# Layer norm of a two-block network: one DVE pass becomes an ACT pass and a POOL product, and an rms scaling goes from POOL to ACT

## The chip, the core and the metric

The kernel runs on one core of a Trainium2 chip. Its time is the device time of one execution in microseconds (us), the median of several runs. The core's engines each work through their own list of instructions in a fixed order and meet by semaphores: TensorE (PE; its weight loads are shown apart as PEld), VectorE (DVE), ScalarE (ACT), GpSimd (POOL) and SyncE (SP), which issues the DMAs.

## What is computed

A sequence of 1024 tokens with 1024 channels, and a context of 256 tokens, go through a "first block" of two layers and then through a "second block". Each layer of the first block projects the tokens, mixes them in three ways (a short convolution, a retention, a windowed attention), multiplies the mixed channels by `w_out`, adds the result, gated, to the scaled input, and takes a layer norm:

```python
def layer_norm(x, g, b):
    xf = x.astype(F32)
    mu = jnp.mean(xf, axis=-1, keepdims=True)
    var = jnp.mean(jnp.square(xf - mu), axis=-1, keepdims=True)
    return ((xf - mu) * lax.rsqrt(var + LN_EPS) * g + b).astype(x.dtype)

x_new = layer_norm(DEEPNORM_ALPHA * x + gate[:, None] * y, ln_g, ln_b)
```

Layer 0 does this for the 1024 tokens and for the 256 context tokens, layer 1 for the 1024 tokens alone. The second block starts with an rms norm of the result, `xf * rsqrt(mean(xf * xf) + RMS_EPS) * g`, and a projection of it.

## The kernel before

Tokens lie in tiles of 128 (partitions) by 1024 (channels), named `tok`: tiles 0 to 3 make group 0, tiles 4 to 7 group 1, and in layer 0 the two context tiles 8 and 9 group 2. Every matmul is made of three fp32r products of high and low halves (`hi`, `lo`); the high half is a copy on ACT or POOL (L211, L213), the low half a difference on DVE (L214, L738).

The stage in question is `p4`. It multiplies by `w_out` in two column halves (`ch`). For each half and each token tile, PE runs 24 matmuls of 128x512 into one PSUM tile `pp` (there are four in rotation); DVE then multiplies by the gate (L1422), adds the scaled input (L1423) and takes the half's statistics (L1429). After the second half `norm` finishes a tile: DVE aggregates mean and variance (L1430), POOL forms `rs`, the inverse root, in two small instructions (L467, L468), and DVE makes two passes over the whole tile (L1432, L1434). `then` stores the tile (`X<-tok`, on SP's queue); in layer 1 it also calls `rms_tok`: a sum of squares on ACT (L754), again L467 and L468 on POOL, and a scaling of the tile in place, on POOL (L1576).

When the last tile of a group is done, `transposes` is put on a background list. Its steps are handed out between matmuls: PE transposes the group's four tiles, one block of 128 channels at a time (four matmuls on L685 into half of a PSUM tile `S`; two such tiles in rotation). Below, k0 to k7 are the eight blocks of a group. In layer 0 ACT evacuates each block with an affine map (L742, into `hv`), POOL makes the high half (L211) and DVE the low half (L214). In layer 1 ACT makes the high half from PSUM (L737) and DVE the low half (L738). A transpose into the second half of an `S` tile waits until the first half has been read: by L742 in layer 0, by L738 in layer 1. `hv` shares its two buffers with the output of L1422.

A scheduler writes each engine's list from the program; within a list the order is fixed.

Of the kernel before, what the change touches and what calls it, by code (L numbers as in the profile page):

```python
# [9 lines left out]
AF = mybir.ActivationFunctionType  # L10
ALU = mybir.AluOpType
# [127 lines left out]
class Kern:  # L139
# [1263 lines left out]
    def p4(s, l, groups, rows):  # L1403

        nc, W = s.nc, s.A["w_out"][l]
        rr = {}
        for ch in range(2):
            wt = s.want("r", W, 0, 8, ch * 512, 512)
            c = slice(ch * 512, (ch + 1) * 512)
            for gi, (act, xsrc, gate, then) in enumerate(groups):  # L1410
                nt = len(xsrc)
                if ch == 0:
                    rr[gi] = [s.tokt() for _ in range(nt)]
                    for t in range(nt):
                        s.load(rr[gi][t], xsrc[t])
                    if not rows:
                        rows += [s.row(s.A["ln_g"][l:l + 1]), s.row(s.A["ln_b"][l:l + 1])]
                r = rr[gi]

                def ev(t, ps):  # L1420
                    y = s.norm.tile([128, 512], F32, tag="hv", name="gy", bufs=2)
                    nc.vector.tensor_tensor(out=y, in0=ps, in1=gate[:, c], op=ALU.mult)  # L1422
                    nc.vector.scalar_tensor_tensor(out=r[t][:, c], in0=r[t][:, c], scalar=ALPHA, in1=y,  # L1423
                                                   op0=ALU.mult, op1=ALU.add)

                def norm(t):
                    st, mv, rs = s.small(12, "bn"), s.small(2, "mv"), s.small(1, "ln")
                    for j in range(2):
                        nc.vector.bn_stats(out=st[:, 6 * j:6 * j + 6], in_=r[t][:, j * 512:(j + 1) * 512])  # L1429
                    nc.vector.bn_aggr(out=mv, in_=st.rearrange("p (j c) -> p j c", j=2))  # L1430
                    s.pow_m05(rs, mv[:, 1:2], 1, 1.0, LN_EPS)
                    nc.vector.scalar_tensor_tensor(out=r[t], in0=r[t], scalar=mv[:, 0:1], in1=rows[0],  # L1432
                                                   op0=ALU.subtract, op1=ALU.mult)
                    nc.vector.scalar_tensor_tensor(out=r[t], in0=r[t], scalar=rs, in1=rows[1], op0=ALU.mult,  # L1434
                                                   op1=ALU.add)
                    then(r, t)
                end = ch == 1 and gi == len(groups) - 1
                s.tm(wt, [(act, t * 128) for t in range(nt)], 512, ev, post=norm if ch else None,
                     outer="t")
# [133 lines left out]
    def rms_tok(s, x):  # L1573

        rs = s.rstd_rms([x], [s.norm.tile([128, 1024], F32, tag="junk", name="junk", bufs=1)])
        s.nc.gpsimd.tensor_scalar(out=x, in0=x, scalar1=rs, scalar2=1.0, op0=ALU.mult, op1=ALU.mult)  # L1576


    def second_block(s, h):
# [505 lines left out]
```

## Time and profile before

| | |
|---|---|
| runs of the kernel before | 3041.79 us median of 3 (3033.36 to 3044.56) |
| the profiled execution | 3042.17 us, of which 3040.0 us lie between its first and last instruction |
| PE, PEld | busy 97% and 80% of the span |
| DVE, ACT, POOL | busy 60%, 34% and 24% |
| `p4` of layer 0, second column half | begins near 786 us; its tiles are done near 877 us |
| `p4` of layer 1, second column half | begins near 1467 us; its tiles are done near 1540 us |
| L1432 and L1434 | 18 instructions each (10 tiles in layer 0, 8 in layer 1) |
| L1576 | 8 instructions |

The profile shows one execution. Times count from the start of its span. An engine's idle time is put down to what released it; a "wait" is idle time before an instruction, with the engine and line that ended it.

### The profile page before, as it was taken

Reading aid. Unit: us, or ns where it says so; the run is one execution under the profiler, and the core shown is the slowest. Engines: PE = TensorE matmul, PEld = TensorE weight load, DVE = VectorE, ACT = ScalarE, POOL = GpSimd, SP = SyncE. Lnnn points to the kernel's source line nnn. Section 1 sums busy time; section 2 is a strip of 40 time slices with the busy share of each in tenths; the row PEclk is TensorE's granted clock in tenths of the full one; section 3 lists DMA queues with packets and bytes.
Section 4 is the critical chain, followed back from the end, with each engine's and each line's share of the span. In section 5 each row is a group of like instructions: output and inputs, shape, how many; then the busy total and the mean of one; then the engine's idle time right before and its main releaser. Section 6 shows DMA issues by size and latency. Waiting matters only on the chain. (4 is left out here: it accounts for less than half of the span.)

```text
span 3040.0 us, 40710 instructions
## 1 busy us (share of the span) xinstructions
PE 2934.0 (97%) x15449; PEld 2445.2 (80%) x15449; DVE 1823.8 (60%) x2813; ACT 1044.3 (34%) x1822; POOL 719.5 (24%) x742
## 2 busy tenths in 40 slices
PE   7989999999999999999999999999899999999989
PEld 5978887787789997887778878788778888887877
DVE  4555643445865644445752376884448877778965
ACT  3222223234122323234121152533454443444462
POOL 3222221121233222121310021212143332224130
PEclk9999999999999999999999999999999999999999
DMA  7273434333433223333312222165453332267554
GB/s 265 60 187 96 120 114 110 112 84 101 168 97 110 83 67 95 89 84 106 140 57 70 87 75 82 63 224 204 137 183 106 116 121 88 84 229 258 172 201 137
DMA packets 343603, 378.47 MB, mean 124 GB/s; under 512 B 30916, under 2 KB 258416, under 8 KB 343408
## 3 DMA queue, kind: packets, MB, share of 16 engines
q1 hardware_dynamic: 343408, 375.87, 39.0%
q8 instruction: 122, 2.00, 0.3%
q14 instruction: 73, 0.60, 0.1%
HBM read 303.11 MB, written 68.76 MB: 122 GB/s over the span
## 5 line engine op out<-in xcount | busy, mean ns | idle before, releaser
L308 PE MATMUL pp<-act_hi,whi 128*128 128x512 f32 (+1 forms) x1472 | 576.1, 392 | 1.6 <-POOL whi L211 1.0
L308 PE MATMUL pp<-act_hi,wlo 128*128 128x512 f32 (+1 forms) x1472 | 562.8, 383 | 1.7 <-DVE wlo L214 1.7
L308 PE MATMUL pp<-act_lo,whi 128*128 128x512 f32 (+1 forms) x1472 | 561.5, 382 | 1.0 <-DVE act_lo L1662 1.0
L214 DVE TENSOR_TENSOR wlo<-wr,whi 128x1024 fp32r<-128x1024 f32 (+2 forms) x304 | 335.1, 1116 | 348.7 <-ACT whi L213 174.7
L308 PE MATMUL pp<-whi,act_hi 128*128 128x384 f32 (+1 forms) x1216 | 446.7, 368 | 26.4 <-ACT pl L1895 9.1
L308 PE MATMUL pp<-wlo,act_hi 128*128 128x384 f32 (+1 forms) x1216 | 442.5, 364 | 4.6 <-DVE wlo L214 4.6
L308 PE MATMUL pp<-whi,act_lo 128*128 128x384 f32 (+1 forms) x1216 | 437.9, 360 | 0.0
L211 POOL TENSOR_SCALAR whi<-wr 128x1024 fp32r<-128x1024 f32 (+2 forms) x128 | 147.3, 1151 | 861.5 <-PE pp L308 610.1
L308 PEld LDWEIGHTS pp<-act_hi,whi 128*128 128x128 f32 x1472 | 278.3, 189 | 73.7 <-issue 20.3
L308 PEld LDWEIGHTS pp<-act_hi,wlo 128*128 128x128 f32 x1472 | 278.7, 189 | 57.3 <-issue 2.7
L308 PEld LDWEIGHTS pp<-act_lo,whi 128*128 128x128 f32 x1472 | 279.1, 190 | 51.0 <-issue 2.5
L213 ACT ACTIVATE whi<-wr 128x1024 fp32r<-128x1024 f32 (+2 forms) x176 | 152.8, 881 | 354.5 <-PE pp L308 267.1
L308 PEld LDWEIGHTS pp<-whi,act_hi 128*128 128x128 f32 x1216 | 231.6, 191 | 51.8 <-issue 11.1
L308 PEld LDWEIGHTS pp<-wlo,act_hi 128*128 128x128 f32 x1216 | 232.3, 191 | 28.0 <-DVE wlo L214 10.3
L308 PEld LDWEIGHTS pp<-whi,act_lo 128*128 128x128 f32 x1216 | 231.7, 191 | 18.0
L1360 POOL TENSOR_SCALAR P<-P,sm 128x640 f32<-128x640 f32 x96 | 76.4, 810 | 223.7 <-DVE sm L1358 223.7
L374 PE MATMUL pp<-act,wx 128*128 128x512 f32 x320 | 124.6, 389 | 0.0
L377 PE MATMUL pp<-act,wx 128*128 128x512 f32 x320 | 124.5, 389 | 0.0
L376 PE MATMUL pp<-act,wx 128*128 128x512 f32 x320 | 124.5, 389 | 0.0
L2036 PE MATMUL pp<-whi,act 128*128 128x512 f32 x384 | 121.5, 394 | 0.0
L1356 ACT ACTIVATE P<-P,sm 128x640 f32<-128x640 f32 x96 | 79.0, 824 | 121.2 <-DVE sm L1354 121.1
L96 POOL TENSOR_TENSOR ws<-wr 128x512 f32<-128x512 f32 x48 | 66.8, 1392 | 153.5 <-DMA wr<-in_w_up_dram 142.8
(378 smaller groups left out, 5237.6 us busy)
## 6 DMA issues: line engine op xcount, KB each, us to landing
wr<-in_w_in_dram SPq DMA_DIRECT2D x40, 768.0 KB
wr<-in_w_up_dram SPq DMA_DIRECT2D x56, 512.0 KB
wr<-in_w_in_dram SPq DMA_DIRECT2D x52, 512.0 KB
wr<-in_w_down_dram SPq DMA_DIRECT2D x21, 1024.0 KB
act<-HID SPq DMA_DIRECT2D x84, 256.0 KB
wr<-in_w_in_dram SPq DMA_DIRECT2D x19, 1024.0 KB
wr<-in_w_mod_dram SPq DMA_DIRECT2D x16, 1024.0 KB
wr<-in_w_out_dram SPq DMA_DIRECT2D x12, 1024.0 KB
```

Of the source, the lines that this page charges most:

```text
L96: s.K.nc.gpsimd.tensor_tensor(out=t, in0=a, in1=b, op=op)
L211: nc.gpsimd.tensor_scalar(out=hi, in0=src, scalar1=1.0, scalar2=0.0, op0=ALU.mult, op1=ALU.add)
L213: nc.scalar.activation(out=hi, in_=src, func=AF.Copy)
L214: nc.vector.tensor_tensor(out=lo, in0=src, in1=hi.bitcast(F32), op=ALU.subtract)
L308: s.nc.tensor.matmul(out=ps, lhsT=lhs[a], rhs=rhs[b], start=first and n == 0, stop=last and n == 2)
L374: s.nc.tensor.matmul(out=ps, lhsT=x[0][:, k], rhs=y[k][0], start=first and k == 0, stop=False, skip_group_check=True)
L376: s.nc.tensor.matmul(out=ps, lhsT=x[0][:, k], rhs=y[k][1], start=False, stop=False, skip_group_check=True)
L377: s.nc.tensor.matmul(out=ps, lhsT=x[1][:, k], rhs=y[k][0], start=False, stop=last and k == 3, skip_group_check=True)
L1356: nc.scalar.activation(out=P[:, hh], in_=P[:, hh], func=AF.Exp, scale=-1.0, bias=m[:, hh:hh + 1], accum_out=sm[:, hh:hh + 1])
L1360: nc.gpsimd.tensor_scalar(out=P[:, hh], in0=P[:, hh], scalar1=sm[:, hh:hh + 1], scalar2=0.5, op0=ALU.mult, op1=ALU.mult)
L2036: nc.tensor.matmul(out=ps[t], lhsT=a[:, c], rhs=b, start=own and k == 0 and n == 0, stop=k == KT - 1 and n == 2, skip_group_check=True)
```

## The change

In `norm` the two DVE passes become four steps. A small DVE instruction forms `mr = -mean * rs` (L1433 of the changed kernel); ACT computes `r * rs + mr` over the tile (L1435); POOL multiplies by the row `ln_g` (L1436); DVE adds the row `ln_b` (L1437). All three passes work in place. In `rms_tok` the scaling of the tile moves from POOL to ACT (L1578).

```diff
                     s.pow_m05(rs, mv[:, 1:2], 1, 1.0, LN_EPS)
-                    nc.vector.scalar_tensor_tensor(out=r[t], in0=r[t], scalar=mv[:, 0:1], in1=rows[0],
-                                                   op0=ALU.subtract, op1=ALU.mult)
-                    nc.vector.scalar_tensor_tensor(out=r[t], in0=r[t], scalar=rs, in1=rows[1], op0=ALU.mult,
-                                                   op1=ALU.add)
+                    mr = s.small(1, "mr")
+                    nc.vector.scalar_tensor_tensor(out=mr, in0=mv[:, 0:1], scalar=-1.0, in1=rs, op0=ALU.mult,
+                                                   op1=ALU.mult)
+                    nc.scalar.activation(out=r[t], in_=r[t], func=AF.Identity, scale=rs, bias=mr)
+                    nc.gpsimd.tensor_tensor(out=r[t], in0=r[t], in1=rows[0], op=ALU.mult)
+                    nc.vector.tensor_tensor(out=r[t], in0=r[t], in1=rows[1], op=ALU.add)
                     then(r, t)
...
         rs = s.rstd_rms([x], [s.norm.tile([128, 1024], F32, tag="junk", name="junk", bufs=1)])
-        s.nc.gpsimd.tensor_scalar(out=x, in0=x, scalar1=rs, scalar2=1.0, op0=ALU.mult, op1=ALU.mult)
+        s.nc.scalar.activation(out=x, in_=x, func=AF.Copy, scale=rs)
```

The lists of DVE, ACT and POOL change around these steps. First DVE, in the run of tiles 1 to 5 of either layer, where one tile's rows repeat for the next. Before, from the statistics of one tile to those of the next:

```order
L1430 BN_AGGR sm<-sm 128x2
L1432 SCALAR_TENSOR_TENSOR tok<-tok,sm,row 128x1024
L1434 SCALAR_TENSOR_TENSOR tok<-tok,sm,row 128x1024
L1422 TENSOR_TENSOR gy<-pp,row 128x512
L1423 SCALAR_TENSOR_TENSOR tok<-tok,gy 128x512
L1429 BN_STATS sm<-tok 128x6
L1430 BN_AGGR sm<-sm 128x2
```

Now:

```order
L1430 BN_AGGR sm<-sm 128x2
L1433 SCALAR_TENSOR_TENSOR sm<-sm 128x1
L1422 TENSOR_TENSOR gy<-pp,row 128x512
L1437 TENSOR_TENSOR tok<-tok,row 128x1024
L1423 SCALAR_TENSOR_TENSOR tok<-tok,gy 128x512
L1429 BN_STATS sm<-tok 128x6
L1430 BN_AGGR sm<-sm 128x2
```

Only L1422 of the next tile has come ahead of the finished tile's last pass L1437; L1423, L1429 and L1430 of the next tile stand behind it.

Second, ACT in layer 0, from the second column half of `p4` to the evacuation of group 0's transposes (`hv` is that evacuation, `whi` a weight's high half):

```order
-L742 ACTIVATE hv<-S,MODC_156 128x512 x4
+L1435 ACTIVATE tok<-tok,sm 128x1024 x5
+L742 ACTIVATE hv<-S,MODC_156 128x512
+L1435 ACTIVATE tok<-tok,sm 128x1024
+L742 ACTIVATE hv<-S,MODC_156 128x512 x3
```

The evacuation of block k0 now stands behind the affine pass of tile 4, and that of k1 to k3 behind the pass of tile 5.

Third, DVE in layer 1, where the low halves of group 0's blocks (`act_lo`) begin. Before:

```order
L1432 SCALAR_TENSOR_TENSOR tok<-tok,sm,row 128x1024
L1434 SCALAR_TENSOR_TENSOR tok<-tok,sm,row 128x1024
L738 SCALAR_TENSOR_TENSOR act_lo<-S,COL,act_hi 128x512
L1422 TENSOR_TENSOR gy<-pp,row 128x512
L1423 SCALAR_TENSOR_TENSOR tok<-tok,gy 128x512
L738 SCALAR_TENSOR_TENSOR act_lo<-S,COL,act_hi 128x512 x2
```

Now:

```order
L1433 SCALAR_TENSOR_TENSOR sm<-sm 128x1
L738 SCALAR_TENSOR_TENSOR act_lo<-S,COL,act_hi 128x512
L1437 TENSOR_TENSOR tok<-tok,row 128x1024
L738 SCALAR_TENSOR_TENSOR act_lo<-S,COL,act_hi 128x512 x2
L1422 TENSOR_TENSOR gy<-pp,row 128x512
```

The low half of k0 stands behind L1433 of tile 5 instead of L1434 of tile 5, and the low halves of k1 and k2 behind L1437 of tile 5.

## Rows read from the trace of the kernel before

**Rows 1.** The page, part 1: busy time, share and instructions by engine

```profile
PE 2934.0 (97%) x15449; PEld 2445.2 (80%) x15449; DVE 1823.8 (60%) x2813; ACT 1044.3 (34%) x1822; POOL 719.5 (24%) x742
```

**Rows 2.** Busy time by stretch: length, each engine's busy us (instructions), granted clock, DMA

```profile
800.00:820.00 20.00, 20.00 (x90) 16.54 (x89) 16.68 (x21) 0.00 (x0) 6.60 (x8) 1.00 0.20 80
```

**Rows 3.** Who waited for whom, 780 to 880 us: total us, times, longest

```profile
PE S L685 <- ACT hv L742: 5.0, 3, 1.8
```

**Rows 4.** The same view, 1465 to 1560 us

```profile
PE S L685 <- DVE act_lo L738: 6.6, 2, 5.1
```

**Rows 5.** Instructions in order of time, DVE, layer 0: start, length, instruction, [idle before]

```profile
793.59 0.21 DVE L1430 BATCH_NORM_AGGREGATE sm<-sm 128x2 f32<-128x12 f32 x1
...
797.52 0.69 DVE L1423 SCALAR_TENSOR_TENSOR tok<-tok,gy 128x512 f32<-128x512 f32 x1
...
798.97 0.21 DVE L1430 BATCH_NORM_AGGREGATE sm<-sm 128x2 f32<-128x12 f32 x1
...
812.47 1.28 DVE L1434 SCALAR_TENSOR_TENSOR tok<-tok,sm,row 128x1024 f32<-128x1024 f32 x1 [0.72 <-POOL sm L468]
```

**Rows 6.** The same view, PE, layer 0: transposes k0, k1, k3 and k7 of group 0

```profile
820.43 0.60 PE L685 MATMUL S<-ident,tok 128*128 128x128 f32 x4
...
821.90 0.66 PE L685 MATMUL S<-ident,tok 128*128 128x128 f32 x4
...
827.52 0.66 PE L685 MATMUL S<-ident,tok 128*128 128x128 f32 x4 [1.76 <-ACT hv L742]
...
838.23 0.66 PE L685 MATMUL S<-ident,tok 128*128 128x128 f32 x4 [1.60 <-ACT hv L742]
```

**Rows 7.** Line L1434, layer 0 (780 to 830 us): count, ns min/median/max, first and last start

```profile
L1434 DVE SCALAR_TENSOR_TENSOR tok<-tok,sm,row x6: 1283/1285/1286, 795.6 to 823.7; 128x1024 f32<-128x1024 f32 x6
```

**Rows 8.** The same view, layer 1 (1465 to 1512 us)

```profile
L1434 DVE SCALAR_TENSOR_TENSOR tok<-tok,sm,row x6: 1285/2148/2159, 1477.3 to 1508.9; 128x1024 f32<-128x1024 f32 x6
```

**Rows 9.** Instructions in order of time, POOL, layer 1

```profile
1479.92 0.19 POOL L467 TENSOR_SCALAR sm<-sm 128x1 f32<-128x1 f32 x1 [2.64 <-ACT junk L754]
...
1480.19 0.56 POOL L468 TENSOR_TENSOR sm<-sm,mhalf 128x1 f32<-128x1 f32 x1
...
1481.04 1.28 POOL L467 TENSOR_SCALAR sm<-sm 128x1 f32<-128x1 f32 x1 [0.29 <-DVE sm L1430]
...
1482.94 1.12 POOL L1576 TENSOR_SCALAR tok<-tok,sm 128x1024 f32<-128x1024 f32 x1
```

**Rows 10.** Single lines elsewhere in the kernel, with the shapes nearest to the new ones

```profile
L1747 ACT ACTIVATE tok<-tok,sm x8: 1147/1152/1157, 2095.8 to 2205.0; 128x1024 f32<-128x1024 f32 x8
...
L1744 DVE TENSOR_TENSOR fx<-fx,acc x8: 1212/1221/1226, 2895.0 to 2954.9; 128x1024 f32<-128x1024 f32 x8
...
L756 DVE TENSOR_TENSOR sm<-sm x24: 147/153/990, 2089.9 to 3008.2; 128x1 f32<-128x1 f32 x24
...
L906 POOL TENSOR_TENSOR d<-d,g x18: 992/1015/1037, 138.4 to 1120.1; 128x384 f32<-128x384 f32 x18
...
L813 POOL TENSOR_TENSOR r<-kr,wk x32: 822/832/1603, 239.6 to 993.9; 128x384 f32<-128x384 f32 x32
...
L124 POOL TENSOR_TENSOR wr<-wr,hid x12: 1282/1738/1746, 2703.6 to 2732.9; 128x512 f32<-128x512 f32 x12
```

**Rows 11.** Instructions in order of time, DVE and ACT, layer 1

```profile
1475.30 0.21 DVE L1430 BATCH_NORM_AGGREGATE sm<-sm 128x2 f32<-128x12 f32 x1
...
1478.68 1.06 ACT L754 ACTIVATE junk<-tok 128x1024 f32<-128x1024 f32 x1 [9.94 <-DVE tok L1434]
...
1511.00 0.74 DVE L738 SCALAR_TENSOR_TENSOR act_lo<-S,COL,act_hi 128x512 fp32r<-128x512 f32 x1
```

**Rows 12.** The same view, PE, layer 1: end of transposes k0, then k1 and k2

```profile
1503.58 0.33 PE L685 MATMUL S<-ident,tok 128*128 128x128 f32 x1 [0.24 <-POOL tok L1576]
...
1511.80 1.97 PE L685 MATMUL S<-ident,tok 128*128 128x128 f32 x8 [5.13 <-DVE act_lo L738]
```

**Rows 13.** Busy time by stretch, after that wait (columns as in rows 2)

```profile
1512.00:1514.00 2.00, 2.00 (x10) 1.90 (x10) 1.36 (x3) 1.21 (x4) 1.25 (x2) 0.50 0.59 242
```

## The prediction

> **What bounds the kernel now.** The page's busy times come first: PE is busy for 2934.0 of 3040.0 us [rows 1], so a change on DVE, ACT or POOL counts only where it makes PE wait, or ends a wait. The table of stretches shows a full stage: 90 matmul records in 20 us at full granted clock [rows 2], about 5.4 us for a token tile's 24 matmuls (20/90 x 24 = 5.3; a few records are missing). Next come PE's waits around the two places the change touches. In layer 0 they sum to 5.0 us, for ACT's evacuation of transposes [rows 3]; in layer 1 to 6.6 us, for DVE's low halves [rows 4]. So in these two stages the change could win back some 12 us and no more, while what it adds to PE's waits has no such limit. The timelines tell what the waits hang on. After a tile's L1430 at 793.80 us (793.59 + 0.21), DVE has finished tile 3 at 813.75 [rows 5], and PE transposes group 0 from 820.43 on [rows 6]: 6.7 us to spare. In layer 1 the spare is gone: PE waits 0.24 us for the last scaled tile, and then 5.13 us because the low half of k0, on DVE at 1511.00, stands behind a whole tile's norm [rows 11, 12].
>
> **What goes.** 18 pairs of passes on DVE. A tile in layer 0 took (813.75 - 793.80 - 1.3 - 1.3 - 0.7)/3 = 5.6 us from L1430 to L1430 (taken off: the two passes of tile 3 and the 0.7 between them), hardly more than PE's 5.4. In layer 1 the second pass takes 2.15 us at the median instead of 1.29 [rows 7, 8], since POOL's scaling (1.12 us) runs at the same time [rows 9]; that overlap goes too.
>
> **What comes, and in which order.** The added instructions are cheap in busy time, but the order of DVE's list makes them one closed loop: L1437 of a tile stands ahead of L1423 of the next, and L1437 waits for DVE, POOL, DVE, ACT and POOL in turn. From the end of L1430 to the end of L1437:
> - L467 and L468 on POOL, undisturbed: 0.27 us from start to start and 0.56, together 0.83 [rows 9];
> - L1433: 0.15, from the 128x1 operation L756 [rows 10];
> - L1435 on ACT: 1.15, from L1747, also 128x1024 with a scale by partition [rows 10];
> - L1436 on POOL: no row has a 128x1024 product. The nearest is L906, an in-place product of 128x384 at 1.015 us, which scales to 2.7. Below it, L813 (0.832 for 384) gives 2.2; above it, L124 (1.738 at the median for 512) gives 3.5. I take 2.7;
> - L1437 on DVE: 1.22, from L1744 [rows 10];
> - five hand-overs of 0.03 to 0.09 us, as between the end of the first L1434 of layer 1, 1477.3 + 1.29 us, and L754's start at 1478.68 [rows 8, 11]: about 0.3.
>
> Together 6.36 us. L1423, L1429 and L1430 of the next tile then take 1.66 us (797.52 to 799.18) [rows 5]. The loop is **8.0 us** a tile, against 5.6 before and PE's 5.4; DVE mostly idles in it.
>
> **Layer 0.** Tile 1 has its L1422 in the loop too (0.7). Tile 3 is done at 793.80 + 6.36 + 3 x 8.02 + 0.7 = 824.9, and PE, ready at 820.43, waits 4.5 us. Block k1 waits for the evacuation of k0, which stands on ACT behind the affine pass of tile 4: L1430 of tile 4 ends at 824.9 + 1.7 = 826.6, its L1435 2.3 us later at 828.9, the evacuation 0.87 later (in rows 6 k1 starts 1.47 after k0, 0.60 of it the transposes). So k1 comes at 829.8, 7.9 late. Block k3 waits for the evacuation of k2, behind that of k1, behind the affine pass of tile 5: 834.6 + 2.3 + two evacuations of 0.8 = 838.6, where it was 827.52: 11.1 late. POOL's product of tile 5 also stands ahead of k1's high half, and `hv` has two buffers; I put k7 at 12.5 late (11 to 14). The four last tiles (6 and 7, context 8 and 9) lose some 2 us each from L1430 to the end. Work by the other tiles lies beside that, so I count 1 us for all (0 to 4). **Layer 0: +13.5.**
>
> **Layer 1.** L1430 of tile 0 ends at 1475.51 [rows 11]. From tile 2 on POOL has the rms root of the tile before (1.24 us from L754's start to L467, then 0.83) [rows 9, 11] ahead of the root for the norm: +0.5 a tile, 8.5 in all. Tile 3 is done at 1507.7. Its scaling on ACT, L1578, stands behind the affine pass of tile 4 (done at 1512.1) and ends 1.15 later: k0's last transpose at 1513.3 instead of 1503.58 [rows 12], 9.8 late. The low half of k0 stands behind L1433 of tile 5 (1517.8 + 0.5 + 1.1 = 1519.4) and takes 0.74, so k1 comes at 1520.2 instead of 1511.80 [rows 12]: 8.4 late, the old 5.13 us already made up for. The second old wait of 1.5 us (6.6 - 5.1) [rows 4] partly falls away. **Layer 1: +7.5.** The eight scalings cost POOL nothing now and ACT 8 x 1.15 us, on an engine at 34% [rows 1]; they hurt only by their place in ACT's list, counted here. The eight stores before them are the same DMAs on SP; none is added.
>
> **Clock.** After the 5.13 us wait, PE's granted clock stood at 0.50, the lower of its two levels (1.2 GHz) [rows 13]; some eight matmuls there took 0.2 us more each, 1.7 us. Layer 1 now has a longer wait, layer 0 three or four of 3 to 5 us close together: +2 (0 to 4).
>
> **Sum.** 13.5 + 7.5 + 2 = 23 us on the profiled execution's 3042.17, which lies 0.4 above the median: **3065 us**. Elsewhere PE waits little, so I expect little of it back later.
>
> The Trainium skill, "GPSIMD Engine Reference", section "Performance versus the Vector engine", keeps elementwise work on VectorE and gives 4497 ns for a 2048-element product-like add, by estimate 2.25 us for 1024. By that price the loop would be 7.6 us and the sum about 3061. The rows on both sides (2.2 and 2.7) leave that open.
>
> **Rivals.**
> 1. *The first waits use up the later ones.* If the product takes 2.2 us, tile 3 is 1.9 us earlier in each layer; and PE, late already at k0, finds ACT and DVE caught up at k1 to k7. Then layer 0 costs about 4.5 and layer 1 about 4.5 (9.8 less the old 5.13): 3051. For it: before, k3 and k7 waited only 1.8 and 1.6 [rows 6]. Against it: the loops of tiles 4 and 5 stand on ACT ahead of those blocks. Chance 0.24.
> 2. *Relief of DVE wins.* The loop stops hurting where the product takes under 1.6 us (4.5 us over four products, 2.7 - 1.1); at DVE's 1.22 the waits of [rows 3] go (-5.0), and layer 1 gains 4 (k0 late by 3.9, 6.6 and 1.7 saved): 3033. Against it: no POOL row of two inputs scales below 2.2. Chance 0.07.
> 3. *Product and DVE exclude each other.* POOL's L467 takes 1.28 us beside a DVE pass, 0.19 without [rows 9], and L1434 is 0.86 longer beside L1576 [rows 7, 8]. In tiles 1 to 5 DVE idles during the product, so this costs nothing there; beside the six last products (tiles 6 to 9 and 6, 7) DVE has other work, and 6 x 2.7 = 16 us of it would be held up, perhaps half of it on PE's path: +8, 3073; with a product of 3.5, 3080. Chance 0.17. The Trainium skill, "SBUF — State Buffer", section "SBUF: two separate sides", says so: a DVE operation with two SBUF inputs and a GpSimd operation that reads SBUF take turns, each for its whole length. Those rows agree.
>
> That the change is not what it says can be left out: the lists hold the 18 new steps and the 8 moved ones.
>
> **How the numbers follow.** Forecast 0.52, with a range of its own of 3055 to 3074. The range for all cases, 3047 to 3080, takes in rivals 1 and 3 and leaves out rival 2 and the edges. A measurement tells about 0.5% from no change (15 us: 3027 to 3057). Slower by more: rival 3 and nearly all of the forecast, 0.67. Within: rival 1, 0.04 of rival 2 and a little of the forecast, 0.30. Faster: 0.03.
>
> **What would show it.** Right: L1437 repeats every 8.0 to 8.5 us in tiles 1 to 4 with DVE idle before it, released by POOL's L1436 at 2.7 us; PE waits 4 to 5 us at k0 and again at k1 and k3 in layer 0, and about 9 us at k0 in layer 1; the rest of the kernel is shifted, not changed. Wrong: a product under 1.6 us, or PE's sum of waits from 780 to 880 us below 10 us.

## The result, and the profile after

The changed kernel takes 3070.41 us, the median of 4 runs (3067.3 to 3071.69), against 3041.97 of 4 runs of the kernel before: a ratio of 1.0101, 95% interval 1.0085 to 1.0117. It is slower by 1.0%, 28 us; forecast were 23. The profiled execution took 3067.3 us, 3065.5 of them between its first and last instruction.

The page's busy times, to be held against [rows 1]:

```profile
PE 2935.4 (96%) x15449; PEld 2445.7 (80%) x15449; DVE 1804.6 (59%) x2813; ACT 1074.0 (35%) x1848; POOL 733.5 (24%) x752
```

DVE lost 19 us of work, ACT and POOL gained 30 and 14, and none of this tells why the kernel is slower. That is read from the two stages, each cut so that PE has the same number of matmul records in it. The table of stretches for the kernel before (columns as in [rows 2]), layer 0 and then layer 1:

```profile
785.00:905.00 120.00, 114.64 (x586) 98.59 (x586) 86.96 (x112) 27.75 (x41) 44.17 (x51) 1.00 0.31 106
1465.00:1600.00 135.00, 128.18 (x568) 102.00 (x567) 92.94 (x115) 36.14 (x55) 38.26 (x45) 0.97 0.20 71
```

The same work in the changed kernel:

```profile
783.27:925.75 142.48, 120.66 (x586) 102.71 (x586) 82.10 (x112) 39.59 (x51) 57.17 (x61) 0.95 0.26 89
1486.17:1628.90 142.73, 129.92 (x568) 102.13 (x567) 77.52 (x115) 54.38 (x71) 38.71 (x45) 0.95 0.19 68
```

Layer 0 is 22.5 us longer: PE's idle time went from 5.4 to 21.8 (+16.5), and the same 586 records keep it busy 6.0 us longer, at a lower granted clock. Layer 1 is 7.7 us longer: 6.0 of idle time and 1.7 of busy time. Together 30.2 us; the span grew by 25.5. The difference of 4.7 lies outside the stages: the changed kernel is 1.7 us shorter ahead of the first L1430 and 3.4 shorter behind the last transpose of layer 1, and 0.4 longer between the layers. I take it for scatter: over the 14 executions profiled in this study that L1430 starts between 789.43 and 794.51 us, although the changes begin only there, and the part behind that transpose lasts from 1479.0 to 1483.5 us, longest in the kernel before.

Who waited for whom, PE, changed kernel, 783 to 926 us, to be held against [rows 3]:

```profile
PE S L685 <- ACT hv L742: 14.2, 5, 3.8
PE pp L308 <- DVE wlo L214: 4.8, 5, 1.7
PE S L685 <- DVE tok L1437: 2.8, 1, 2.8
```

The same for 1486 to 1629 us, against [rows 4]:

```profile
PE S L685 <- ACT tok L1578: 8.5, 2, 7.8
PE S L685 <- DVE act_lo L738: 3.7, 3, 2.6
PE pp L308 <- ACT act_hi L737: 0.6, 1, 0.6
```

The loop is there. Instructions in order of time, DVE, layer 0, against [rows 5]:

```profile
800.28 0.21 DVE L1430 BATCH_NORM_AGGREGATE sm<-sm 128x2 f32<-128x12 f32 x1
801.45 0.16 DVE L1433 SCALAR_TENSOR_TENSOR sm<-sm 128x1 f32<-128x1 f32 x1 [0.95 <-POOL sm L468]
805.39 1.23 DVE L1437 TENSOR_TENSOR tok<-tok,row 128x1024 f32<-128x1024 f32 x1 [3.18 <-POOL tok L1436]
807.98 0.21 DVE L1430 BATCH_NORM_AGGREGATE sm<-sm 128x2 f32<-128x12 f32 x1
```

From one L1430 to the next it is 7.7 us, and DVE stands idle for 4.1 of them. The new steps by line, whole kernel (ns min/median/max):

```profile
L1435 ACT ACTIVATE tok<-tok,sm x18: 1240/1244/1249, 793.2 to 1561.0; 128x1024 f32<-128x1024 f32 x18
L1436 POOL TENSOR_TENSOR tok<-tok,row x18: 2344/2390/3051, 794.5 to 1562.3; 128x1024 f32<-128x1024 f32 x18
L1437 DVE TENSOR_TENSOR tok<-tok,row x18: 1211/1226/2054, 797.0 to 1564.7; 128x1024 f32<-128x1024 f32 x18
```

PE's transposes of group 0, against [rows 6]; the waits are those of k0's last matmul, k1, k3 and k5:

```profile
822.00 0.33 PE L685 MATMUL S<-ident,tok 128*128 128x128 f32 x1 [2.81 <-DVE tok L1437]
826.62 1.12 PE L685 MATMUL S<-ident,tok 128*128 128x128 f32 x4 [3.36 <-ACT hv L742]
...
835.33 0.66 PE L685 MATMUL S<-ident,tok 128*128 128x128 f32 x4 [3.12 <-ACT hv L742]
...
843.48 0.66 PE L685 MATMUL S<-ident,tok 128*128 128x128 f32 x4 [3.80 <-ACT hv L742]
```

And the table of stretches around the first of these waits:

```profile
820.00:824.00 4.00, 1.25 (x5) 0.74 (x5) 2.73 (x4) 0.00 (x0) 1.00 (x3) 0.94 0.31 126
824.00:828.00 4.00, 1.38 (x6) 1.29 (x7) 0.76 (x2) 1.91 (x2) 2.45 (x2) 0.50 0.01 5
828.00:832.00 4.00, 4.00 (x16) 3.09 (x14) 2.73 (x4) 0.00 (x0) 0.99 (x3) 0.70 0.32 131
```

After the waits for k0 and k1 PE runs at 0.50, the lower of its two levels (1.2 GHz).

### The profile page after: what moved, and what is told of

It is laid out like the page before. It is cut to its first block, busy times and chain, and to the rows that moved or that the text cites. A ratio compares the mean times of both kernels' runs of the same rounds, so it can differ in the third digit from the quotient of the medians.

```text
span 3065.5 us, 40746 instructions
## 1 busy us (share of the span) xinstructions
PE 2935.4 (96%) x15449; PEld 2445.7 (80%) x15449; DVE 1804.6 (59%) x2813; ACT 1074.0 (35%) x1848; POOL 733.5 (24%) x752
## 5 line engine op out<-in xcount | busy, mean ns | idle before, releaser
L308 PEld LDWEIGHTS pp<-whi,act_hi 128*128 128x128 f32 x1216 | 232.2, 191 | 49.8 <-issue 10.6
```

The lines of the kernel that those rows point to most:

```text
L308: s.nc.tensor.matmul(out=ps, lhsT=lhs[a], rhs=rhs[b], start=first and n == 0, stop=last and n == 2)
```

## The experiments

All are compared with runs of the kernel before on the same chip (medians 3039.2 us for runs 1 to 4, 3038.48 for runs 5 to 8 and 3037.31 for runs 9 to 12). Since a gain in one place can hide a loss in another, a second yardstick is taken from each trace: the time from the first L1430 of a layer to the start of its last transposes (layer 0: the context tiles', layer 1: group 1's). Before it is 893.07 - 793.59 = 99.48 us and 1556.14 - 1475.30 = 80.84 us; the table gives the differences. The rows for layer 0, first the end in the kernel before, then start and end in the changed kernel (913.82 - 791.86 = 121.96):

```profile
893.07 0.44 PE L685 MATMUL S<-ident,tok 128*128 128x128 f32 x2
...
791.86 0.21 DVE L1430 BATCH_NORM_AGGREGATE sm<-sm 128x2 f32<-128x12 f32 x1
...
913.82 0.44 PE L685 MATMUL S<-ident,tok 128*128 128x128 f32 x2
```

Where a layer's code is that of the kernel before, they stay within 0.3 us (runs 1, 3, 4), so they can be trusted to about that.

| run | new norm in | what else | ratio of times, 95% interval | layer 0, us | layer 1, us |
|---|---|---|---|---|---|
| the change | all tiles | scaling on ACT | 1.0101 (1.0085 to 1.0117) | +22.5 | +7.7 |
| 1 | none | scaling on ACT | 0.9970 (0.9958 to 0.9982) | -0.3 | -6.6 |
| 2 | all tiles | scaling on POOL | 1.0110 (1.0090 to 1.0130) | +22.3 | +9.8 |
| 3 | layer 0 | scaling on POOL | 1.0070 (1.0050 to 1.0091) | +22.5 | 0.0 |
| 4 | layer 1 | scaling on ACT | 1.0019 (1.0007 to 1.0032) | -0.2 | +7.9 |
| 5 | all tiles | shift deferred | 1.0046 (1.0030 to 1.0062) | +18.7 | -2.1 |
| 6 | tiles 6 to 9 | scaling on ACT | 1.0013 (1.0001 to 1.0026) | +10.6 | -5.4 |
| 7 | tiles 0 to 5 | scaling on ACT | 1.0055 (1.0037 to 1.0072) | +12.8 | +5.8 |
| 8 | all tiles | product on DVE | 1.0008 (0.9997 to 1.0020) | +7.7 | -3.7 |
| 9 | tiles 6 to 9 | product on DVE | 0.9988 (0.9978 to 0.9997) | +4.2 | -6.8 |
| 10 | tiles 6 to 9 | product and shift on POOL | 1.0044 (1.0031 to 1.0056) | +15.0 | -1.0 |
| 11 | tiles 0 to 3 | scaling on ACT | 1.0037 (1.0025 to 1.0050) | +10.0 | +2.1 |
| 12 | tiles 0 to 3 | shift deferred | 1.0013 (1.0004 to 1.0023) | +5.6 | -1.9 |

Runs 5 to 12 all have the scaling on ACT, so in layer 1 they are to be held against run 1's -6.6, the old norm with that scaling.

**Runs 1 to 4: the parts and the layers.** The theory: the closed loop costs the time. The rival for layer 1: the scaling on ACT does. Run 1 keeps the old norm and takes the second part of the diff alone:

```diff
-        s.nc.gpsimd.tensor_scalar(out=x, in0=x, scalar1=rs, scalar2=1.0, op0=ALU.mult, op1=ALU.mult)
+        s.nc.scalar.activation(out=x, in_=x, func=AF.Copy, scale=rs)
```

> Only the second part of the change: the two DVE passes of the norm stay, the rms scaling of layer 1 goes from POOL to ACT. Theory (the cost of the change is the closed loop of the norm, the scaling is free): no loop, so no cost; L1434 in layer 1 gets its 0.86 us back, since POOL no longer reads a tile beside it, and PE's wait of 5.1 us in layer 1 shrinks by one to three us: 3038 to 3042 us. Rival (the scaling on ACT is what costs layer 1 its time, because it queues there): PE waits longer for the scaled tiles, 3046 us or more.

Measured: 3028.65 us, 10.6 less than before and below the expected range. This part is a gain, and the kernel with it alone beats both others. Line L1434 of run 1, layer 1, to be held against [rows 8]:

```profile
L1434 DVE SCALAR_TENSOR_TENSOR tok<-tok,sm,row x6: 1283/1284/1286, 1470.8 to 1498.9; 128x1024 f32<-128x1024 f32 x6
```

And DVE's first low half there, in order of time, against [rows 11]:

```profile
1500.12 0.74 DVE L738 SCALAR_TENSOR_TENSOR act_lo<-S,COL,act_hi 128x512 fp32r<-128x512 f32 x1
```

The pass is back from 2.15 to 1.28 us with POOL's scaling gone, and k0's low half comes 31.6 us after the layer's first L1430 (1468.54) instead of 35.7. PE's longest wait there fell from 5.1 to 1.5 us. The stretch with the same 568 records, in run 1:

```profile
1458.24:1586.62 128.38, 125.49 (x568) 99.92 (x567) 87.43 (x115) 45.15 (x63) 27.97 (x37) 1.00 0.21 75
```

PE's idle time in it was 6.8 us and is now 2.9, and PE is busy 125.49 us instead of 128.18, at a granted clock of 1.00 instead of 0.97. So k0's low half came four microseconds earlier, and PE got 6.6 back. That is what the trace shows of the 10.6 us; the rest has no place in it, and the interval (5.5 to 12.8 us) allows 6.6 alone.

Run 2 takes the first part alone (norm changed, scaling still on POOL):

> Only the first part of the change: affine on ACT, product on POOL, shift on DVE, while the rms scaling stays on POOL. Theory: nearly the whole loss stays, 3065 to 3072 us; the scaling now queues behind products on POOL instead of affine passes on ACT. Rival (the scaling on ACT costs layer 1 its time): the loss of layer 1 goes, 3062 us or less.

Measured 3072.22 us: the whole loss stays and the rival falls. In layer 1 it is 2 us worse than the change: the scaling waits behind products on POOL for longer than behind affine passes on ACT.

Runs 3 and 4 put the new code behind a condition:

```diff
+                    if l == 0:
```

> The new norm in layer 0 alone; layer 1 as in the kernel before, scaling on POOL. From the shifts in the two traces (the context tiles' transposes come 22.5 us later) theory says +22: 3064 us, with the same PE waits between 780 and 895 us as in the changed kernel. The terms of the prediction as they stood say +14 to +16: 3057 us.

> The new norm and the scaling on ACT in layer 1 alone; layer 0 as in the kernel before. Theory: +6 us, 3048, with a PE wait of about 8 us at k0 (for the scaled tile) in place of the 5.1 us at k1. The terms of the prediction say +7.5 to 9: 3050 us. If the two layers do not add up to the loss of the whole (28 us), they act on one another, or something between them costs time.

Measured 3060.96 and 3046.39 us, 21.8 and 7.2 over the kernel before: the two layers add up to the loss of the whole. Layer 0's +22.5 is the change's own, to the tenth, and layer 1's +7.9 is close to it; the wait for the scaled tile in run 4 is 8.5 us, as in the change. The two parts of the change don't add up in layer 1: the norm alone costs 9.8 there (run 2) and the scaling alone gives 6.6 (run 1), but beside the new norm the scaling gives only 2.1 (from +9.8 to +7.7), so that the norm costs 14.3 when the scaling is on ACT already.

**Run 5: the loop opened.** The shift of a tile takes a factor of one formed from the next tile's mean, so it stands behind the next tile's statistics:

```diff
+                    one = s.small(1, "mr")
+                    nc.vector.tensor_scalar(out=one, in0=mv[:, 0:1], scalar1=0.0, scalar2=1.0, op0=ALU.mult, op1=ALU.add)
...
-                    nc.vector.tensor_tensor(out=r[t], in0=r[t], in1=rows[1], op=ALU.add)
-                    then(r, t)
+                    late.append(t)
+                    while late and (len(late) > 1 or t == nt - 1):
+                        p = late.pop(0)
+                        nc.vector.scalar_tensor_tensor(out=r[p], in0=r[p], scalar=one, in1=rows[1], op0=ALU.mult,
+                                                       op1=ALU.add)
+                        then(r, p)
```

> All passes as in the changed kernel, on the same engines, but the shift of a tile takes a factor of one that DVE forms from the next tile's mean, so that it can only stand behind the next tile's L1430 (the last tile of a group is shifted at once). One small DVE instruction of 0.15 us a tile is added. Theory (the loop costs the time: DVE's list makes the next tile's statistics wait for ACT and POOL): a tile takes PE's 5.4 to 5.6 us again, tile 3 is done near 817 us, the waits for the evacuations fall to what they were before, and the time to 3036 to 3046 us. Rival (the product on POOL takes time from DVE beside it, or ACT's affine passes in front of the evacuations cost it, whatever the order): products and passes are all still there and more of them lie beside DVE's work, so 3058 us or more.

Measured 3050.84 us, between the two: half of the loss goes. The wait for k0 in layer 0 went, and layer 1 is 2.1 us shorter than before, 9.8 less than in the change; but layer 0 kept 18.7. Theory and rival each had a part, and the next runs separate them by tiles.

**Runs 6 and 7: early and late tiles.** In tiles 0 to 5 DVE has nothing else to do during the product; in the later ones it makes low halves of weights (`wlo`) and of group 0's blocks.

```diff
+                    if 4 * gi + t >= 6 or len(groups) == 1:
```

> The new norm only for the tiles beside which DVE has other work: 6 to 9 of layer 0, 6 and 7 of layer 1; the old norm for tiles 0 to 5, scaling on ACT. Theory (the loop of tiles 0 to 5 costs the time): 3040 to 3046 us. Rival (product and DVE exclude each other in the last six tiles, so that low halves of weights come late): 10 to 16 us of loss, 3052 us or more.

> The reverse: the new norm for tiles 0 to 5 of each layer, the old norm for the rest, scaling on ACT. Theory: nearly the whole loss, 3062 to 3070 us. Rival (the last six tiles cost 10 us or more by themselves): 3058 us or less.

Measured 3041.57 and 3054.12 us. Run 6's number lies in the theory's range, but only because the scaling's gain, unknown when it was written, lies in it too: against run 1 it is 12.9 us of loss, as the rival said, and layer 0 shows 10.6 of it with no help from the scaling. Run 7 is where the rival put it. The two nearly add up: 10.6 + 12.8 = 23.4 in layer 0, for the change's 22.5. The stretch of layer 0 in run 7, with the same 586 records:

```profile
782.68:915.50 132.82, 120.01 (x586) 102.41 (x586) 81.30 (x112) 34.87 (x47) 49.62 (x57) 0.95 0.28 95
```

What the late tiles lose, DVE, run 6, tiles 6 and 7:

```profile
844.34 2.06 DVE L1438 TENSOR_TENSOR tok<-tok,row 128x1024 f32<-128x1024 f32 x1 [1.56 <-POOL tok L1437]
...
848.13 0.99 DVE L1434 SCALAR_TENSOR_TENSOR sm<-sm 128x1 f32<-128x1 f32 x1
849.04 0.68 DVE L1423 SCALAR_TENSOR_TENSOR tok<-tok,gy 128x512 f32<-128x512 f32 x1
849.64 4.54 DVE L214 TENSOR_TENSOR wlo<-wr,whi 128x1024 fp32r<-128x1024 f32 x2
```

POOL at the same time (its line numbers are one higher than the change's):

```profile
847.40 1.71 POOL L211 TENSOR_SCALAR whi<-wr 128x1024 fp32r<-128x1024 f32 x1
850.48 2.61 POOL L1437 TENSOR_TENSOR tok<-tok,row 128x1024 f32<-128x1024 f32 x1 [1.37 <-ACT tok L1436]
```

Two low halves that take 1.21 us each at the median took 4.54: the second one lasts from 850.8 to 854.2, through the rest of the product (850.48 to 853.09) and 1.1 us more. PE's waits follow:

```profile
PE S L685 <- ACT hv L742: 7.7, 5, 2.1
PE pp L308 <- DVE wlo L214: 5.4, 5, 1.7
```

**Runs 9 and 10: is it the product beside DVE, or DVE waiting for it?** DVE's list also waits for the product (1.56 us above, 6.9 in all for the four late tiles of layer 0) in front of low halves. Run 9 makes the late tiles' product on DVE (the first two lines below), run 10 makes both product and shift on POOL (the last two), so that DVE waits for neither:

```diff
-                        nc.gpsimd.tensor_tensor(out=r[t], in0=r[t], in1=rows[0], op=ALU.mult)
+                        nc.vector.tensor_tensor(out=r[t], in0=r[t], in1=rows[0], op=ALU.mult)
...
-                        nc.vector.tensor_tensor(out=r[t], in0=r[t], in1=rows[1], op=ALU.add)
+                        nc.gpsimd.tensor_tensor(out=r[t], in0=r[t], in1=rows[1], op=ALU.add)
```

> As the run with the new norm in the late tiles alone (3041.6 us, 13 above the run with the scaling on ACT and the old norm, 3028.7), but with the late tiles' product on DVE: POOL has none. Rival, now the favourite for the late tiles (product on POOL and work on DVE hold each other up): nearly all of the 13 us goes, 3028 to 3034 us, and the two low halves of weights that took 4.5 us take 2.4 to 2.8. Other reading (DVE's list waits for ACT and POOL in front of the low halves): ACT's pass is still in the chain, so half of it or more stays, 3036 us or more.

> The new norm in the late tiles alone, with product and shift both on POOL: DVE has neither and waits for nothing of the chain. If DVE's waits in front of the low halves cost the 13 us, they go: 3028 to 3034 us. If product and DVE hold each other up, POOL now has two passes of 2.4 us or more a tile beside DVE's low halves: 3040 us or more, with low halves of 4 us and over.

Measured 3034.01 and 3050.58 us. Giving DVE more work cost less (+4.2 in layer 0 instead of +10.6), giving it less cost more (+15.0). So 6.4 of the 10.6 us hang on the product being on POOL. The low halves of weights (`wlo`) between 822 and 880 us in runs 1, 6 and 9, in this order (ns min/median/max):

```profile
L214 DVE TENSOR_TENSOR wlo<-wr,whi x12: 947/1212/1639, 827.7 to 859.7; 128x1024 fp32r<-128x1024 f32 x8, 128x768 fp32r<-128x768 f32 x4
L214 DVE TENSOR_TENSOR wlo<-wr,whi x12: 903/1213/3401, 829.1 to 870.6; 128x1024 fp32r<-128x1024 f32 x8, 128x768 fp32r<-128x768 f32 x4
L214 DVE TENSOR_TENSOR wlo<-wr,whi x12: 945/1210/1636, 827.2 to 861.5; 128x1024 fp32r<-128x1024 f32 x8, 128x768 fp32r<-128x768 f32 x4
```

DVE in run 10:

```profile
850.03 0.99 DVE L1434 SCALAR_TENSOR_TENSOR sm<-sm 128x1 f32<-128x1 f32 x1 [3.18 <-POOL sm L468]
...
853.27 2.79 DVE L214 TENSOR_TENSOR wlo<-wr,whi 128x1024 fp32r<-128x1024 f32 x1 [0.53 <-ACT whi L213]
857.00 3.37 DVE L214 TENSOR_TENSOR wlo<-wr,whi 128x1024 fp32r<-128x1024 f32 x1 [0.94 <-POOL whi L211]
```

POOL beside it:

```profile
852.38 2.61 POOL L1437 TENSOR_TENSOR tok<-tok,row 128x1024 f32<-128x1024 f32 x1 [1.36 <-ACT tok L1436]
...
856.94 2.36 POOL L1438 TENSOR_TENSOR tok<-tok,row 128x1024 f32<-128x1024 f32 x1
```

Each of the two low halves ends 1.1 us after the POOL pass beside it: it ran when that was over. The longest took 3.37 us, less than the 4 expected. In run 9 the 1024-wide low halves from 845 us on take 1.21 us each. The Trainium skill, "SBUF — State Buffer", section "SBUF: two separate sides", has the rule: a DVE operation with two SBUF inputs and a GpSimd operation that reads SBUF exclude each other for their whole length. The traces agree. But run 10's +15.0 is not exclusion alone: PE waits 2.4 us for a high half that queues behind passes on POOL, and DVE, which was to wait for nothing, stands idle 3.18 us for the root L468, which queues on POOL behind product and shift of tile 6. And run 9 takes away both the exclusion and DVE's wait for the product. So how the 6.4 us are shared between the two is not shown; run 9's remaining 4.2 us (5.4 in time) were not taken apart either.

**Run 8: the loop shorter, POOL free.** All tiles new, but the product on DVE:

> Affine on ACT, but product and shift both on DVE, so POOL has no product. Theory: the loop is shorter by the product's 2.39 less DVE's 1.22 us, 6.5 us a tile instead of 7.65, still over PE's 5.4: tile 3 is done near 819 us, in time, but the evacuations of k0 to k3 still stand behind the affine passes of tiles 4 and 5, a few us late; 3046 to 3052 us. Rival (only POOL's product beside DVE costs time): nothing left of the loss, 3042 us or less.

Measured 3041.02 us: as the rival had it by the time, but for another reason again, the scaling's gain. Layer 0 is 7.7 longer than before: the loop is 6.2 to 7.2 us a tile, and PE still waits 8.2 us for the evacuations in 7 pieces. Of the change's 22.5 us in layer 0, 14.8 hang on the product being on POOL.

**Runs 11 and 12: group 0 alone.** The new norm for tiles 0 to 3, without and with the shift deferred:

```diff
+                    if gi == 0 and len(groups) > 1:
```

> The new norm for tiles 0 to 3 of each layer alone, old norm from tile 4 on, scaling on ACT. No product and no affine pass is left beside the evacuations. Theory (the loop makes tile 3 some 8 us late, and DVE, which needs 5.6 us a tile itself, cannot catch up, so that the low halves of group 0 come late): about 10 us in each layer on top of 3028.7, 3045 to 3053 us. Rival (products and affine passes of tiles 4 and 5 in front of the evacuations on POOL and ACT are what costs): 3036 us or less.

> The same tiles, with the shift tied behind the next tile's statistics as in the run without the loop. Theory: no loop and nothing in front of the evacuations, so nothing is left of the loss: 3026 to 3034 us. If it stays above 3040 us, something else in the new steps costs time in tiles 0 to 3.

Measured 3047.49 us for run 11, in the range of the theory: +10.0 in layer 0, +8.7 over run 1 in layer 1, without any product or affine pass near the evacuations. Run 12 took 3041.64, more than expected: my theory was incomplete. DVE in run 12, layer 0:

```profile
811.03 1.28 DVE L1445 SCALAR_TENSOR_TENSOR tok<-tok,sm,row 128x1024 f32<-128x1024 f32 x1 [1.29 <-POOL tok L1441]
813.03 0.16 DVE L1438 SCALAR_TENSOR_TENSOR sm<-sm 128x1 f32<-128x1 f32 x1 [0.71 <-POOL sm L468]
...
816.98 1.28 DVE L1445 SCALAR_TENSOR_TENSOR tok<-tok,sm,row 128x1024 f32<-128x1024 f32 x1 [3.19 <-POOL tok L1441]
...
827.50 1.63 DVE L1451 SCALAR_TENSOR_TENSOR tok<-tok,sm,row 128x1024 f32<-128x1024 f32 x1 [0.71 <-POOL sm L468]
829.05 1.69 DVE L214 TENSOR_TENSOR act_lo<-hv,act_hi 128x512 fp32r<-128x512 f32 x2
```

And its transposes k3:

```profile
831.07 1.12 PE L685 MATMUL S<-ident,tok 128*128 128x128 f32 x4 [6.37 <-ACT hv L742]
```

Two things are left. A tile takes 5.95 us (811.03 to 816.98), since the small root on POOL is held up beside the shift (L467 takes 1.28 us there, as in [rows 9]) and the next product hangs on it; and tile 3 is still shifted at once, with DVE idle for 3.19 us. Tile 3 is done at 818.3, in time for k0. But the old norm of tiles 4 and 5 needs DVE for 5.6 us a tile, which is more than PE's 5.4, so DVE can't catch up, and the low half that frees a buffer of `hv` for the evacuation of k2, for which k3 waits, stands behind tile 5. This is how a late tile 3 is paid for, in run 11 too (k3 waits 6.21 us there).

## Why the prediction was right, and where it was not

- **What bounds the kernel**: right. The loss lies in PE's waits and in PE's longer busy time at a lower granted clock, although DVE had 19 us less to do.
- **The loop of 8.0 us**: right, 7.7 measured. L1433 took 0.16 (0.15 taken), the shift 1.23 (1.22), the product 2.39 (2.7 taken, between bounds of 2.2 and 3.5), the affine pass 1.24 (1.15). The Trainium skill, "GPSIMD Engine Reference", section "Performance versus the Vector engine", gave 2.25 for the product by estimate: nearer than my row, and still below the measured value. In layer 1 8.2 us a tile (8.5).
- **Layer 0, tiles 0 to 5: +12.5**: right in size, +12.8 in run 7. Tile 3 was done at 821.95, 29.9 us after the first L1430 (31.1 forecast). The last block, k7, came 13.0 us late in run 7 (12.5 forecast). In idle time it is only 7.5 us (12.8 against 5.4): the rest, 5.4, is PE's longer busy time. When a block comes is set by DVE, POOL and ACT, so what PE runs slower meanwhile comes out of its wait.
- **Layer 0, the last four tiles: +1 (0 to 4)**: this step failed. It is +9.7 in the change (22.5 - 12.8) and +10.6 alone. "Work by the other tiles lies beside that" overlooked that DVE's work there is held up by a product on POOL, or waits for it: 6.4 of the 10.6 hang on that (run 9), and the other 4.2 stay open. Rival 3 had the mechanism and nearly the size (+8, "perhaps half of it on PE's path"), but as an alternative to the forecast instead of a part of it.
- **Layer 1: +7.5**: the sum is right (+7.7), its steps only roughly. k0 came 8.5 us late (9.8 forecast) and k1 6.4 (8.4); then the lateness grew again, where the forecast let it shrink. The forecast wait of about 9 us at k0 was 8.5, in two pieces. The overlap of POOL's scaling with DVE's second pass was named ("that overlap goes too") and given no number: with the scaling on ACT layer 1 is 6.6 us shorter beside the old norm (run 1) and 2.1 beside the new one (the change against run 2).
- **Clock: +2 (0 to 4)**: PE's busy time grew by 7.7 us for the same records. In layer 0 this was no term on top of the lateness: with k7 13.0 us late, run 7's stage ends 12.8 us late, so most of the slower running is counted in the lateness already. In layer 1 it may be part of the 1.3 us by which the lateness grows from k1 to the end; that was not separated. Run 1, where 2.7 us of busy time went along with 3.9 us of waiting, shows that the clock can come on top.
- **Sum**: 12.5 + 1 + 7.5 + 2 = 23 forecast; 12.8 + 9.7 + 7.7 = 30.2 in the two stages, less 4.7 outside them in the profiled execution. The median of 3070.41 is 5 us above the forecast: the late tiles' missing 8.7 us, partly covered by the clock term and by what lies outside the stages.
- **Rivals**: 1, waits used up by the first, fell: k1, k3 and k5 each waited over 3 us. (Its sum left out its own condition: with tile 3 earlier by 1.9 us in each layer, 3051 would have been about 3047.) 2, relief of DVE, fell; run 8, with a product of 1.23 us, still leaves +7.7 in layer 0, though there DVE carries it; a product as fast as that on POOL was not tried. 3 is true beside the forecast.
- **Signs**: L1437 came every 7.7 us in layer 0, a little under the 8.0 to 8.5 named, and the waits at k0, k1 and k3 were 2.8, 3.4 and 3.1 us, under the 4 to 5 named. "Shifted, not changed" failed in the late tiles. Neither sign of being wrong came: the product took 2.39 us, and PE's waits from 780 to 880 us sum to 18.9.

## What to carry to other kernels

A pass that is handed from one engine to two others is not priced by its busy time: if the list of the first engine waits for the result ahead of the next tile's work, the chain becomes the pace of the loop, here 7.7 us instead of 5.6. Before moving elementwise work to POOL, look at what DVE does meanwhile: DVE work with two SBUF operands can grow by nearly the whole length of a POOL pass beside it (a low half by 2.2 us beside a pass of 2.36 in run 10). Try the parts of a change apart and together: here one alone cost 33 us and the other alone gave 10.6, but beside the first the second gave only 2.1 of its 6.6 us in layer 1.

## What had not been expected

- Moving eight scalings of 1.1 us from POOL to ACT, which looked neutral, saves 10.6 us (0.3%) beside the old norm. The trace places 6.6 of it in layer 1, where DVE's second pass no longer has POOL's scaling beside it. This version is the fastest of the study at 3028.65 us.
- A single 128x1 instruction on DVE took 0.99 us instead of 0.16 beside POOL work, and a product of 2.39 us took up to 3.05.
- A wait that is removed can give back more than its length: run 1 took 3.9 us of idle time out of layer 1 and 2.7 us of PE's busy time with it, as the granted clock of the stage went from 0.97 to 1.00.
